# Two neighbouring rows to a partition: a matrix product with rotary embedding, rows 2p and 2p+1 of 256 in place of row 4p+r of 512

## The chip, the cores and the metric

One core of a Trainium2 chip runs the kernel. The metric is the device time of one execution in microseconds (us). Engines: PE (matmul; PEld is its loading of weights), DVE, ACT, POOL, and SP, which here only issues transfers. ACT and POOL issue transfers too; each engine works through its own instructions in order.

## The reference

x is 16 x 512 x 768 in float32, the weight 768 x 768, cos and sin 512 x 64. With 12 heads of 64 columns, the kernel computes a product and rotates it by position:

```python
y = np.matmul(x, weight)                       # (16, 512, 768)
y = y.reshape(batch, seq, n_heads, head_dim)   # head_dim 64
y1, y2 = y[..., :32], y[..., 32:]
out1 = y1 * cos1 - y2 * sin1                   # cos1, sin1: first 32 columns of cos, sin
out2 = y2 * cos2 + y1 * sin2                   # cos2, sin2: the other 32; indexed by the position in seq
out = np.concatenate([out1, out2], axis=-1).reshape(batch, seq, hidden)
```

## The kernel before

**Tiles and groups.** The 8192 rows of x are cut into 64 tiles of 128 rows, four tiles to a group, 16 groups (0 to 15, `LAST` is 15). Tile s of group g is, of batch 4*(g//4)+s, the rows 4p + g%4 for p = 0 to 127 (`where`). So all tiles of a group have the same positions and need the same row of cos and sin on each partition. A load or a store of a tile moves 128 rows of 768 floats (3 KB), each 12 KB from the next.

**From x to the product.** PE needs x transposed, in fp16. For most tiles SP loads a tile to `xs` (L210), ACT casts it to `xc` with the columns sorted into three blocks of pairs (`cast`, the copy of L190), PE transposes it through PSUM (`turn_rows`, L271; in the start-up `turn`, L256), and ACT copies the result to `xt` (L190). These are the plain tiles. In groups 5 to 13 and in group 15 the second pair of tiles of the group is a block (`BLOCKS`): four quarter loads bring 32-row pieces of it (`load_quarter`, L225) so that a transposition of 32x32 squares on DVE (`turn_pair`, L299) turns both tiles at once into `xp`. Blocks of odd groups come by SP to `xb` and are cast by ACT to `xd` (`cast_pair`); blocks of groups 6, 8, 10 and 12 come by POOL, which casts in the transfer, to `xh`, and DVE then reads them with a step of three words. PE takes the transposed tile as its weights and streams the weight matrix past it, into six PSUM banks `py` (3072 columns, one group). From tile 4 to tile 57 it works with half arrays: two streams of 64 rows each (`walk`, `one`, L362), the second 1024 columns behind the first, so that both halves of the array are busy; the start-up and the end use the whole array (L337).

**Rope.** A group's 3072 columns are cut into units: 0 to 512, 512 to 1536, 1536 to 2048, 2048 to 3072 (in the last groups into units of 512, at the very end of 256 and 128). For each unit DVE multiplies the product once with cos and once with the shifted sin (`rope`, L419; `csn` holds both, with a broadcast over the heads of a unit) and POOL adds the two halves into `ov` (L445). A finished unit frees its banks for the next group. From group 1 on POOL adds both units of a half group at once (128x1536).

**Order.** Everything is emitted in a fixed order by the loop over tiles i. At the end of step i it emits DVE's turn of a block that is due (`bturns`), PE's transposition of tile i+3 and ACT's copy of it (`turns`), ACT's cast of tile i+5 (`casts`), POOL's loads, and the stores that are due (`stores`, L477, most on ACT's queue, the last ones on SP's). `pump` emits loads on SP's queue as buffers come free: ten buffers `xs` of one tile, three of a block. Semaphores alone decide when an instruction starts; an instruction that waits holds back all behind it on its engine.

Of the kernel before, what the change touches and what calls it, by code (L numbers as in the profile page):

```python
# [10 lines left out]
FP32 = mybir.dt.float32  # L11
# [97 lines left out]
def kernel(  # L109
# [19 lines left out]
    R = 32  # L129
    NQ = P // R  # L130
    NT = H // (2 * P)
    SB = S // P
    QB = 4
    NG = B * SB // QB
# [10 lines left out]
    def sbuf(name, shape, dt):  # L145
        return nc.alloc_sbuf_tensor(name, shape, dt).ap()

    NX, NB, NBH, NC, NCP, NXT, NXP, NOV = 10, 3, 3, 5, 2, 8, 4, 4

    ident = sbuf("ident", [P, P], FP16)  # L150
    cold = sbuf("cold", [P, 512], FP16)
    sin_sb = sbuf("sin_sb", [P, SB, D], FP32)
    csn = sbuf("csn", [P, 2, SB, D], FP32)
    w_raw = sbuf("w_raw", [P, NT, 2, H], FP32)
    w_sb = sbuf("w_sb", [P, NT, 2, H], FP16)
    xs_b = [sbuf(f"xs{i}", [P, H], FP32) for i in range(NX)]
    xb_b = [sbuf(f"xb{i}", [P, 2 * H], FP32) for i in range(NB)]
    xh_b = [sbuf(f"xh{i}", [P, 2 * H], FP16) for i in range(NBH)]
    xc_b = [sbuf(f"xc{i}", [P, H], FP16) for i in range(NC)]
    xd_b = [sbuf(f"xd{i}", [P, 2 * H], FP16) for i in range(NCP)]  # L160
# [32 lines left out]
    def where(i):  # L193
        g, s = divmod(i, QB)
        return QB * (g // SB) + s, g % SB

# [7 lines left out]


    def load(i, e="sp"):
        b, r = where(i)
        k = ring("xs", NX)
        xs[i] = k
        do(e, lambda eng: eng.dma_start(  # L210
            out=xs_b[k], in_=x[b].rearrange("(p r) h -> r p h", r=SB)[r]),
            writes=[f"xs{k}"], dma=f"xs{k}")

    def load_quarter(gh, q):
        g, h = gh
        b, r = where(g * QB + 2 * h)
        e = BLOCKS[gh]
        src = x[b : b + 2].rearrange("b (j a r) (q k) -> r q a (b j) k", r=SB, a=R, q=NQ)
        if q == 0:
            xs[gh] = ring("xh", NBH) if e == "pool" else ring("xb", NB)  # L220
        k = xs[gh]
        name = f"xh{k}" if e == "pool" else f"xb{k}"
        buf = xh_b[k] if e == "pool" else xb_b[k]
        dst = buf.rearrange("p (j k) -> p j k", j=2 * NQ)
        do(e, lambda eng: eng.dma_start(out=dst[ts(q, R)], in_=src[r, q]),  # L225
           writes=[f"{name}q{q}"], dma=name)

# [13 lines left out]
    def cast(i, e):  # L241
        k = xs[i]
        c = ring("xc", NC)
        xc[i] = c
        do(e, copy(e, xc_b[c].rearrange("p (t m e) -> p t m e", t=NT, e=2),
                   xs_b[k].rearrange("p (m t e) -> p t m e", t=NT, e=2)),
           reads=[f"xs{k}"], writes=[f"xc{c}"])

    def turn(i, e):
        c = xc[i]  # L250
        k = ring("pt", 2)
        z = ring("xt", NXT)
        src = xc_b[c].rearrange("p (t m e) -> p t e m", t=NT, e=2)
        pt = pt_b[k].bitcast(FP16)[:, 0:H].rearrange("p (t e m) -> p t e m", t=NT, e=2)
        for t, h in CHUNKS:
            do("pe", lambda eng: eng.transpose(pt[:, t, h, :], src[:, t, h, :], ident),  # L256
               reads=[f"xc{c}", "ident"], writes=[f"pt{k}"], tick=(t, h) == CHUNKS[-1])
        do(e, copy(e, xt_b[z], pt), reads=[f"pt{k}"], writes=[f"xt{z}"])
        xT[i] = (lambda t, h: xt_b[z][:, t, h, :], f"xt{z}")

    def turn_rows(i, e):

        c = xc[i]
        z = ring("xt", NXT)
        src = xc_b[c].rearrange("p (t m e) -> p t e m", t=NT, e=2)
        pts = [pt_b[r].bitcast(FP16)[:, 0 : H // 2].rearrange(
            "p (t e m) -> p t e m", t=NT, e=2) for r in range(2)]
        for t, h in CHUNKS:
            for r in range(2):
                rows = ts(r, HP)  # L270
                do("pe", lambda eng: eng.transpose(  # L271
                    pts[r][:, t, h, :], src[rows, t, h, :], ident[rows, rows]),
                    reads=[f"xc{c}", "ident"], writes=[f"pt{r}"], tick=(t, h) == CHUNKS[-1])
        do(e, copy(e, xt_b[z].rearrange("p t e (r m) -> p r (t e) m", r=2),
                   pt2.bitcast(FP16)[:, :, 0 : H // 2].rearrange("p r (c m) -> p r c m", m=HP)),
           reads=["pt0", "pt1"], writes=[f"xt{z}"])
        xT[i] = (lambda t, h: xt_b[z][:, t, h, :], f"xt{z}")

    def cast_pair(gh, e="act"):
        k = xs[gh]  # L280
        c = ring("xd", NCP)
        xc[gh] = c
        do(e, copy(e, xd_b[c].rearrange("p (t j e) -> p t j e", t=NT, e=2),
                   xb_b[k].rearrange("p (j t e) -> p t j e", t=NT, e=2)),
           reads=[f"xb{k}q{q}" for q in range(NQ)], writes=[f"xd{c}"])

    def turn_pair(gh):
        g, h = gh
        z = ring("xp", NXP)
        dst = xp_b[z].bitcast(FP32)  # L290
        if BLOCKS[gh] == "pool":
            k = xs[gh]
            src = xh_b[k].bitcast(FP32).rearrange("p (j t) -> p t j", t=NT)
            rd = [f"xh{k}q{q}" for q in range(NQ)]
        else:
            c = xc[gh]
            src, rd = xd_b[c].bitcast(FP32), [f"xd{c}"]
        v = xp_b[z].rearrange("p (t m e) -> p t e m", t=NT, e=2)
        do("dve", lambda eng: eng.transpose(out=dst, in_=src), reads=rd, writes=[f"xp{z}"])  # L299
        for s in (0, 1):  # L300
            xT[g * QB + 2 * h + s] = (
                lambda t, e, s=s: v[:, t, e, ts(s, P)], f"xp{z}")

# [92 lines left out]
    def rope(g, u):  # L396
        c0, c1, ps, banks, adder = u
        w, r = c1 - c0, g % SB
        nh = w // D
        whole = 0 < g and (g, c0 // 1536) < (LAST - 4, 1)  # L400
        if adder == "dve":
# [11 lines left out]
        else:  # L413
# [4 lines left out]
            tq, keys = products(home, 512, 0, 256) if adder == "hold" else products(home, w, 0, w)  # L418
        do("dve", lambda eng: eng.tensor_tensor(  # L419
            out=tq.rearrange("p j (h d) -> p j h d", d=D),  # L420
            in0=ps.rearrange("p (h d) -> p h d", d=D)
            .unsqueeze(1).broadcast_to((P, 2, nh, D)),
            in1=csn[:, :, r, :].unsqueeze(2).broadcast_to((P, 2, nh, D)),
            op=MULT), reads=banks + ["csn"], writes=keys)
        if g not in ov_of:
# [41 lines left out]
    def store(g, c0, c1, e):  # L467

        o = ov_of[g]
        b, r = where(g * QB)  # L470
        s0, s1 = c0 // H, -(-c1 // H)
        dst = out.rearrange("b (p r) h -> r p b h", r=SB)[r, :, b + s0 : b + s1]
        src = ov_b[o].rearrange("p (b h) -> p b h", b=QB)[:, s0:s1]
        if (c1 - c0) % H:
# [3 lines left out]
           reads=[f"ov{o}c{c}" for c in range(c0, c1, 64)],  # L478
           dma=f"xs{c0 // 256 % NX}" if (c1 - c0) % H else f"ov{o}_{c0}")

# [8 lines left out]
    for k in order:  # L489
# [4 lines left out]
    do("sp", lambda eng: eng.dma_start(  # L494
        out=csn[:, 0], in_=cos.rearrange("(p r) d -> p r d", r=SB)), writes=["cos"], dma="ov3_0")
    do("sp", lambda eng: eng.dma_start(
        out=sin_sb, in_=sin.rearrange("(p r) d -> p r d", r=SB)), writes=["sin"], dma="ov3_1536")


    fetch, quarters = [], []  # L500
    soon = [p for p in sorted(BLOCKS) if BLOCKS[p] == "sp"]
    for i in range(QB, NTILE):
        if soon and i >= max(2, soon[0][0] - 1) * QB:
            quarters += [(soon[0], q) for q in (0, 2, 1, 3)]
            soon.pop(0)
        if not is_block(i):
            fetch.append(i)
            for _ in range(2 if i == QB * (LAST - 1) else 1):
                if quarters:
                    fetch.append(quarters.pop(0))  # L510
        elif quarters and quarters[0][0] == pair_of(i):
            fetch.append(quarters.pop(0))
    fetched = [0]
    xs_used, xb_used = [0], [0]
    xs_sent, xb_sent = [4], [0]

    def pump():

        while fetched[0] < len(fetch):
            j = fetch[fetched[0]]  # L520
            if isinstance(j, int):
                if xs_sent[0] - xs_used[0] >= NX:
                    return
                load(j)
                xs_sent[0] += 1
            else:
# [26 lines left out]
    def castx(i, e):  # L553
        cast(i, e)
        xs_used[0] += 1

# [21 lines left out]
    for c in CHUNKS[3:5]:  # L578
# [4 lines left out]
    do("dve", lambda eng: eng.tensor_copy(  # L583
        out=csn[:, 1, :, 0:HD], in_=sin_sb[:, :, HD:D]), reads=["sin"], writes=["csn1"])
    do("dve", lambda eng: eng.tensor_scalar_mul(
        out=csn[:, 1, :, HD:D], in0=sin_sb[:, :, 0:HD], scalar1=-1.0),
        reads=["sin", "csn1", "cos"], writes=["csn"])
    assert not quarters
    pump()
# [164 lines left out]
```

## Time and profile before

| | |
|---|---|
| three runs | 150.62, 150.62, 152.17 us; median 150.62 |
| span of the profiled execution | 148.2 us; its own time is not listed beside it, so what lies outside the span is taken from the median: 2.4 us |
| granted clock of PE | 0.998 |
| moved by the transfers | 51.67 MB in 27555 packets, 349 GB/s on the mean |
| busy share of PE, DVE, ACT, POOL | 95, 85, 53, 82% |

The span runs from the first to the last instruction. "Busy" of PE is a modelled end for each matmul, so it is not a share of its peak. In the lines of groups, the columns are: line, engine, operation, output and input with their shapes, count; then busy us in all, mean ns of one; then the idle time ahead of them and who ended it. A line number can be that of a helper: L190 is the copy for all engines. In a timeline a line has the start in us, the length in us, then what ran; neighbours on an engine overlap in the records by about 0.1 us.

Four windows, in busy us of each engine:

| window | PE | DVE | ACT | POOL | share of the DMA engines |
|---|---|---|---|---|---|
| 0 to 18 us | 14.91 | 8.18 | 9.01 | 1.99 | 0.90 |
| 18 to 52 us | 34.00 | 28.50 | 27.88 | 31.66 | 1.08 |
| 52 to 100 us | 48.00 | 45.92 | 22.63 | 45.16 | 1.12 |
| 100 to 126 us | 26.00 | 24.87 | 14.02 | 24.65 | 1.04 |
| 126 to 148.2 us | 17.89 | 18.55 | 5.51 | 18.30 | 0.81 |

Up to 18 us is the start-up, in 18 to 52 us fall groups 1 to 4, whose tiles are all plain, then come the groups with blocks; the last window is the end.

### The profile page before, as it was taken

How to read it: one execution, taken by the hardware profiler on the slowest of the kernel's cores; microseconds unless marked ns; L12 is line 12 of the kernel's file. 1: busy time of each engine (PE TensorE's matmuls, PEld its weight loads, DVE VectorE, ACT ScalarE, POOL GpSimd, SP SyncE). 2: the span in 40 equal slices, each digit the busy share in tenths (PEclk: the TensorE clock that was granted, in tenths of full speed). 3: DMA queues.
4: the chain of work that ended last, by engine and by line, in shares of the span. 5: the costliest groups of instructions: out<-in, count | busy, mean ns of one | idle time of the engine just before them, and what ended most of it. 6: DMA issues, size and time to landing. Idle time of an engine off the chain costs nothing.

```text
span 148.2 us, 4422 instructions
## 1 busy us (share of the span) xinstructions
PE 140.8 (95%) x1948; PEld 112.7 (76%) x1948; DVE 126.0 (85%) x99; ACT 79.0 (53%) x94; POOL 121.8 (82%) x73
## 2 busy tenths in 40 slices
PE   6789999999999999999999999999999999999980
PEld 2335578888888888888888888888888888765860
DVE  0335998886988899899989998999989999999991
ACT  3453898777777933557261915375263919931010
POOL 1000396999999998999999999879699999999990
PEclk9999999999999999999999999999999999999999
DMA  3999999999999999999999999999999999998675
GB/s 124 352 395 403 402 406 398 373 379 296 317 366 330 352 353 277 294 408 287 319 355 397 379 323 358 365 408 324 381 365 337 411 409 416 410 408 333 264 297 180
DMA packets 27555, 51.67 MB, mean 349 GB/s; under 512 B 6160, under 2 KB 13072, under 8 KB 27536
## 3 DMA queue, kind: packets, MB, share of 16 engines
q1 hardware_dynamic: 15824, 28.84, 57.0%
q10 hardware_dynamic: 7360, 20.97, 35.9%
q0 software_dynamic: 4352, 1.57, 8.6%
q8 instruction: 15, 0.25, 0.7%
q14 instruction: 4, 0.03, 0.1%
HBM read 27.79 MB, written 25.17 MB: 357 GB/s over the span
## 4 chain that ended last, share of the span: by engine, by line
PE 78%; DVE 12%; DMA 4%; issue 1%; SPq 1%; DVEq 0%
PE py L362 68%; DVE tq L419 8%; PE py L337 5%; PE pt L271 4%; DMA w_raw<-in_weight_dram 4%; DVE w_raw L419 2%; SPq L210 1%; PE pt L256 1%; DVE ov L445 1%; DVE xs L419 1%; SPq L232 1%; DVE w_sb L190 0%; DVEq L57 0%; SPq L749 0%; SPq L119 0%
## 5 line engine op out<-in xcount | busy, mean ns | idle before, releaser
L445 POOL TENSOR_TENSOR ov<-tq 128x512 f32<-128x512 f32 (+3 forms) x35 | 76.8, 2220 | 20.1 <-DVE tq L419 20.1
L362 PE MATMUL py<-w_sb,xt 64*128 64x256 f16 (+1 forms) x864 | 81.5, 323 | 0.0
L419 DVE TENSOR_TENSOR tq<-py,csn 128x1024 f32<-128x1024 f32 (+2 forms) x51 | 74.4, 1496 | 4.6 <-PE py L362 4.5
L362 PEld LDWEIGHTS py<-w_sb,xt 64*128 64x128 f16 x864 | 59.9, 94 | 11.1 <-DVE tq L419 0.4
L190 ACT COPY xt<-pt 128x768 f16<-128x768 f16 x42 | 33.5, 801 | 47.5 <-PE pt L271 46.3
L362 PE MATMUL py<-w_sb,xp 64*128 64x512 f16 (+1 forms) x432 | 42.7, 323 | 0.0
L190 ACT CAST xc<-xs 128x768 f16<-128x768 f32 x44 | 38.8, 911 | 6.9 <-DMA xs<-in_x_dram 6.7
L419 DVE TENSOR_TENSOR w_raw<-py,csn 128x1024 f32<-128x1024 f32 (+1 forms) x22 | 35.3, 1606 | 4.4 <-PE py L362 4.0
L445 POOL TENSOR_TENSOR ov<-w_raw 128x1536 f32<-128x1536 f32 (+2 forms) x15 | 35.4, 2374 | 1.9 <-DVE w_raw L419 1.9
L362 PEld LDWEIGHTS py<-w_sb,xp 64*128 64x128 f16 x432 | 30.7, 94 | 5.0
L337 PE MATMUL py<-w_sb,xt 128*128 128x256 f16 (+1 forms) x102 | 17.0, 317 | 1.4 <-DVE w_sb L190 1.1
L271 PEld LDWEIGHTS pt<-ident,xc 64*128 64x128 f16 x456 | 14.9, 95 | 1.3 <-issue 0.2
L337 PEld LDWEIGHTS py<-w_sb,xt 128*128 128x128 f16 x102 | 9.2, 98 | 7.4 <-DVE w_sb L190 2.7
L271 PE MATMUL pt<-ident,xc 64*128 64x64 f16 x456 | 14.7, 190 | 0.0
L190 ACT CAST xd<-xb 128x1536 f16<-128x1536 f32 x6 | 9.8, 1634 | 0.0
L225 POOL DMA_DIRECT2D xh<-in_x_dram x16 | 9.4, 591 | 0.0
L190 DVE CAST w_sb<-w_raw 128x768 f16<-128x768 f32 x6 | 3.4, 559 | 3.6 <-DMA w_raw<-in_weight_dram 3.6
L299 DVE STREAM_TRANSPOSE xp<-xd 128x768 f32<-128x768 f32 x6 | 5.8, 970 | 0.0
L190 ACT COPY ov<-py 128x256 f32<-128x256 f32 x1 | 0.4, 372 | 10.1 <-POOL ov L445 10.1
L540 PE MATMUL py<-cold 128*128 128x512 f16 x12 | 4.3, 521 | 1.4 <-DVE cold L482 1.4
L190 DVE COPY xt<-pt 128x768 f16<-128x768 f16 x2 | 1.1, 558 | 4.8 <-PE pt L256 4.8
L299 DVE STREAM_TRANSPOSE xp<-xh 128x768 f32<-128x768 f32 x4 | 4.9, 1234 | 0.0
(23 smaller groups left out, 22.6 us busy)
## 6 DMA issues: line engine op xcount, KB each, us to landing
out_dram<-ov ACTq DMA_DIRECT2D x26, 768.0 KB, 9.6
xs<-in_x_dram SPq DMA_DIRECT2D x44, 384.0 KB, 16.4
xb<-in_x_dram SPq DMA_DIRECT2D x24, 192.0 KB, 16.4
out_dram<-ov SPq DMA_DIRECT2D x4, 768.0 KB, 6.2
w_raw<-in_weight_dram SPq DMA_DIRECT2D x6, 384.0 KB, 6.9
xh<-in_x_dram POOLq DMA_DIRECT2D x16, 96.0 KB, 12.1
out_dram<-ov SPq DMA_DIRECT2D x1, 384.0 KB, 2.3
out_dram<-ov ACTq DMA_DIRECT2D x1, 384.0 KB, 2.3
```

Of the source, the lines that this page charges most:

```text
L190: eng.copy(out=o, in_=i_) if e == "act" else eng.tensor_copy(out=o, in_=i_)
L210: do(e, lambda eng: eng.dma_start(out=xs_b[k], in_=x[b].rearrange("(p r) h -> r p h", r=SB)[r]), writes=[f"xs{k}"], dma=f"xs{k}")
L225: do(e, lambda eng: eng.dma_start(out=dst[ts(q, R)], in_=src[r, q]), writes=[f"{name}q{q}"], dma=name)
L232: do(e, lambda eng: eng.dma_start(out=w_raw[:, t, h], in_=wv[t, h]), writes=[f"wr{t}{h}"], dma=f"ov{t}_0" if h else f"xb{t}")
L256: do("pe", lambda eng: eng.transpose(pt[:, t, h, :], src[:, t, h, :], ident), reads=[f"xc{c}", "ident"], writes=[f"pt{k}"], tick=(t, h) == ...
L271: do("pe", lambda eng: eng.transpose(pts[r][:, t, h, :], src[rows, t, h, :], ident[rows, rows]), reads=[f"xc{c}", "ident"], writes=[f"pt{r ...
L299: do("dve", lambda eng: eng.transpose(out=dst, in_=src), reads=rd, writes=[f"xp{z}"])
L337: do("pe", lambda eng: eng.matmul(ps, get(t, h), w_sb[:, t, h, a - s * H : z - s * H], start=start, stop=stop), reads=[key, f"w{t}{h}"], w ...
L362: do("pe", lambda eng: eng.matmul(py[:, a:z], get(t, h)[rows], w_sb[rows, t, h, a - s * H : z - s * H], start=start, stop=not opens and en ...
L419: do("dve", lambda eng: eng.tensor_tensor(out=tq.rearrange("p j (h d) -> p j h d", d=D), in0=ps.rearrange("p (h d) -> p h d", d=D) .unsque ...
L445: do(adder, lambda eng: eng.tensor_tensor(out=ov_b[o][:, ds(c0, w)].rearrange("p (h t d) -> p h t d", t=2, d=HD), in0=tq[:, 0].rearrange(" ...
L540: do("pe", lambda eng: eng.matmul(py[:, ts(b, 512)], cold[:, 0:P], cold, start=True, stop=warmed[0] < WARM - 6), reads=["cold"], writes=[f ...
```

## The change

The rows are dealt out anew. Groups 0 to 11 (`NEW` is 12) are now one batch each: tile s of group g holds the rows 256*(s//2) + 2p + s%2 of batch g. Two neighbouring tiles of a pair thus lie in memory as 128 runs of 6 KB. Groups 12 to 15 take four batches (12 to 15) and one tile of each, rows 256*u + 2p + v with u, v = divmod(g-12, 2), as groups of equal positions like before. With that come these edits:

- Pairs 6 to 23 that are no blocks (eleven pairs, tiles 12 to 45) are loaded by one transfer of 6 KB rows (`load_two`) and cast by one instruction on ACT when the second tile of the pair is due (`cast_two`). Pairs 0 to 5 and the pairs of groups 12 to 15 go tile by tile (`by_tile`), as before.
- `xs` and `xc` are buffers of a pair: six and three of them, in place of ten and five of a tile.
- The two halves of a group 0 to 11 are stored as 128 runs of 6 KB (24 stores).
- A block's quarter of groups 5 to 11 is still one transfer; of groups 12, 13 and 15 it is two. The order of rows in a block is another, and DVE's transposition writes its words with a step of 8 words (32 bytes) where it wrote them packed; PE then reads every fourth fp16 of `xp`, where it read every second.
- A unit of 1024 columns in groups 0 to 11 holds 256 columns of an even row and 768 of an odd one. `csn` gets four slots (even, odd, odd, odd) so that one instruction still does a unit; the two further slots are filled by a copy on POOL in the start-up (`csnx`).
- cos and sin are loaded as two runs of 512 B to a partition, before one of 1 KB.

The core of the diff:

```diff
-    NX, NB, NBH, NC, NCP, NXT, NXP, NOV = 10, 3, 3, 5, 2, 8, 4, 4
+    NX, NB, NBH, NC, NCP, NXT, NXP, NOV = 6, 3, 3, 3, 2, 8, 4, 4
...
-    csn = sbuf("csn", [P, 2, SB, D], FP32)
+    csn = sbuf("csn", [P, 2, 2, 4, D], FP32)
...
     def where(i):
         g, s = divmod(i, QB)
-        return QB * (g // SB) + s, g % SB
+        return (g, s) if g < NEW else (NEW + s, g - NEW)
...
+    def by_tile(pr):
+        return pr < 6 or pr >= 2 * NEW
...
+    def load_two(pr, e="sp"):
+        b, r = where(2 * pr)
+        k = xs[pr] = ring("xs", NX)
+        do(e, lambda eng: eng.dma_start(
+            out=xs_b[k], in_=x[b].rearrange("(u p v) h -> u p (v h)", p=P, v=2)[r // 2]),
+            writes=[f"xs{k}_0", f"xs{k}_1"], dma=f"xs{k}_0")
...
+    def cast_two(pr, e):
+        k = xs[pr]
+        c = xc[pr] = ring("xc", NC)
         do(e, copy(e, xc_b[c].rearrange("p (t m e) -> p t m e", t=NT, e=2),
                    xs_b[k].rearrange("p (m t e) -> p t m e", t=NT, e=2)),
-           reads=[f"xs{k}"], writes=[f"xc{c}"])
+           reads=[f"xs{k}_0", f"xs{k}_1"], writes=[f"xc{c}_0", f"xc{c}_1"])
...
     def turn_pair(gh):
...
-        dst = xp_b[z].bitcast(FP32)
+        dst = xp_b[z].bitcast(FP32).rearrange("p (t a w) -> p t w a", t=NT, a=R)
...
-        v = xp_b[z].rearrange("p (t m e) -> p t e m", t=NT, e=2)
+        v = xp_b[z].rearrange("p (t m s e) -> p t e s m", t=NT, s=2, e=2)
         do("dve", lambda eng: eng.transpose(out=dst, in_=src), reads=rd, writes=[f"xp{z}"])
         for s in (0, 1):
             xT[g * QB + 2 * h + s] = (
-                lambda t, e, s=s: v[:, t, e, ts(s, P)], f"xp{z}")
+                lambda t, e, s=s: v[:, t, e, s], f"xp{z}")
...
+        if mixed:
+            make = lambda eng: eng.tensor_tensor(
+                out=tq, in0=ps.unsqueeze(1).broadcast_to((P, 2, w)),
+                in1=csn[:, u].rearrange("p j g d -> p (j g) d")
+                .unsqueeze(2).broadcast_to((P, 8, w // 256, D)), op=MULT)
...
     def store(g, c0, c1, e):
...
+        if g < NEW:
+            dst = out[g].rearrange("(u p v) h -> u p (v h)", p=P, v=2)[c0 // (2 * H)]
+            do(e, lambda eng: eng.dma_start(out=dst, in_=ov_b[o][:, c0:c1]),
+               reads=[f"ov{o}c{c}" for c in range(c0, c1, 64)], dma=f"ov{o}_{c0}")
+            return
...
     def castx(i, e):
-        cast(i, e)
-        xs_used[0] += 1
+        if by_tile(i // 2):
+            cast(i, e)
+        elif i % 2:
+            cast_two(i // 2, e)
+        xs_used[0] += i % 2
...
+    two = csn.rearrange("p u j g d -> p (u j) g d")
+    do("pool", lambda eng: eng.tensor_copy(
+        out=two[:, :, 2:4], in_=two[:, :, 1:2].broadcast_to((P, 4, 2, D))),
+        reads=["csn"], writes=["csnx"])
```

## The prediction, on record before the changed kernel ran

> **What bounds the kernel now.** I read four views in this order: the page, the chain of waits that ended last, the groups by form, and the timelines of ACT and DVE. The page first:
>
> ```profile
> span 148.2 us, 4422 instructions
> PE 140.8 (95%) x1948; PEld 112.7 (76%) x1948; DVE 126.0 (85%) x99; ACT 79.0 (53%) x94; POOL 121.8 (82%) x73
> ...
> PE 78%; DVE 12%; DMA 4%; issue 1%; SPq 1%; DVEq 0%
> ```
>
> PE fills its line, and the chain is PE's for 78% and DVE's for 12%. The page's DMA row is full too (9 in nearly all slices), but only 4% of the chain is a transfer, and that is a load of the weights before 10 us. The chain in order of time shows where PE holds the end:
>
> ```profile
> 31.19 0.17 PE pt L271 x10
> 31.36 1.93 PE py L362 x19
> ...
> 50.49 5.86 PE py L362 x54
> ...
> 125.86 3.45 DVE tq L419 x3
> ```
>
> From 18 to 125.8 us the chain is PE without a gap: one tile of matmuls takes 1.92 to 1.96 us and a transposition 0.17 to 0.20, so a tile period is 2.13 us, or 8.15 us for a group of four of which two are transposed on PE. After 125.86 us DVE sets the end. So time is lost by anything that makes PE wait before 126 us, or DVE late after it; faster transfers gain nothing while nobody waits for them. The longest wait of ACT for x is 2.4 us, and all four such waits lie before 16 us. The rows for what the change touches:
>
> ```profile
> L190 ACT CAST xc<-xs 128x768 f16<-128x768 f32 x44 | 38.8, 911 | 6.9 <-DMA xs<-in_x_dram 6.7
> L419 DVE TENSOR_TENSOR tq<-py,csn 128x2048 f32<-128x2048 f32 x17 | 38.7, 2276 | 0.8 <-PE py L362 0.8
> ...
> L190 ACT CAST xd<-xb 128x1536 f16<-128x1536 f32 x6 | 9.8, 1634 | 0.0
> ...
> L299 DVE STREAM_TRANSPOSE xp<-xd 128x768 f32<-128x768 f32 x6 | 5.8, 970 | 0.0
> L299 DVE STREAM_TRANSPOSE xp<-xh 128x768 f32<-128x768 f32 x4 | 4.9, 1234 | 0.0
> ```
>
> **The change, part by part.** The order of PE's and of DVE's instructions stays as it was, with the same shapes apart from one; what changes is when their inputs come and how they lie.
>
> *The pair cast on ACT (cast_two).* Eleven pairs of groups 3 to 11 are cast by one instruction of 128x1536 instead of two of 128x768. The xd row has that shape and that pattern: 1634 ns against 2 x 911. ACT saves 11 x 0.19 = 2.1 us, worth nothing, since it waits 46 us for PE's transposes. But the even tile's cast moves back, to where the odd tile's stood, and so past one copy xt<-pt. The new order on ACT is: copy of tile 11, cast of 12 and 13, copy of 12, copy of 13, cast of 14 and 15, and so on. Behind the cast stands PE's next transposition, which reads its result, and behind that, in PE's order, all further matmuls. The timeline of ACT before:
>
> ```profile
> 29.32 0.80 ACT L190 COPY xt<-pt 128x768 f16<-128x768 f16 x1 [0.52 <-PE pt L271]
> 30.01 0.90 ACT L190 CAST xc<-xs 128x768 f16<-128x768 f32 x1
> 31.44 0.80 ACT L190 COPY xt<-pt 128x768 f16<-128x768 f16 x1 [0.54 <-PE pt L271]
> ```
>
> The copy of tile 11 starts at 29.32 (copies are the tiles in order, every 2.13 us). A cast starts 0.69 later, at 30.01, and with 1.63 it ends at 31.64; in the start-up PE begins 0.05 after such a cast, so at 31.69. In the timeline of PE the transposition of tile 12 begins at 31.00. PE waits 0.69 us. This happens at each pair whose first transposition follows one tile period after the last one: tiles 12, 14, 16, 18 and 20. From group 6 on the plain pair comes after two tiles that DVE turned, 5.86 us later, and the cast is hidden. 5 x 0.69 = 3.45 us, on PE's line and so on the path. The ends: 0.5 each (2.5 us) if the transposition could in truth start no earlier than 0.25 before its copy (31.19), and 0.75 each (3.75) if the weight load's head start is lost as well.
>
> *The block's transposition on DVE (turn_pair, L299 before).* The same 768 elements are written with consecutive words 32 bytes apart (t, w, a with a innermost) and not packed, ten times. No row has a hop on the written side. The nearest is xh's, which reads with a step of 12 bytes: 1234 against 970 ns, so 8 more bytes of step cost 264 ns. A gain is excluded, packed is the least. So the bounds of one instruction's extra are 0 (a written hop is free) and 264 x 28/8 = 924 ns (in proportion to the step, 28 bytes more). I take the upper, because the price rose with the distance in the only two points there are and 32 is farther out than 12: 970 + 924 = 1894 ns. For xh, which hops on the read side already, I let the longer side count: 1894 - 1234 = 660. Six and four: 6 x 0.924 + 4 x 0.660 = 8.18 us.
>
> What covers it: DVE's own idle time. A group needs two units of 2276 ns and two of half that size, 1217 ns (6.7 us by their starts) and the transposition, in 8.15 us. After each of the first eight transpositions DVE waits for PE once, for 0.54, 0.26, 0.41, 0.27, 0.54, 0.15, 0.54 and 0.28 us, 2.99 in all. After the last two there is nothing left:
>
> ```profile
> 119.17 0.97 DVE L299 STREAM_TRANSPOSE xp<-xd 128x768 f32<-128x768 f32 x1
> 120.06 1.19 DVE L419 TENSOR_TENSOR tq<-py,csn 128x1024 f32<-128x1024 f32 x1
> 121.17 3.83 DVE L419 TENSOR_TENSOR w_raw<-py,csn 128x1024 f32<-128x1024 f32 x3
> 124.95 0.98 DVE L299 STREAM_TRANSPOSE xp<-xd 128x768 f32<-128x768 f32 x1
> 125.86 6.98 DVE L419 TENSOR_TENSOR tq<-py,csn 128x1024 f32<-128x1024 f32 x6
> ```
>
> Then the units come late, PE waits for the banks that they free, and since DVE makes the end, what is not swallowed is paid in full: 8.18 - 2.99 = 5.19 us. At xh's price (0.264 each) the first eight fit and only the last two are paid, 0.5 us; at the full 0.924 for all ten it is 6.3.
>
> A page speaks against this edit. The Trainium skill, "Vector Engine (DVE) Microarchitecture Reference", section "5.2 Measured stream behaviour on trn2", has a written stream that steps 24 words each element at 2.50 ns per column against about 1.05 packed, and says that small steps cost more than large ones. By the rows the edit costs 5.19 us; by that figure an estimate is 768 x 1.45 = 1.11 us each, 8.1 us after the same idle time, and 162.5 us for the kernel. The trace agrees with its rule that a hop costs; its figure for a written one no run here shows.
>
> *Weights from xp.* PE now reads the turned block with 8 bytes between columns, 4 before. xt (packed) and xp (4 bytes) both take 94 ns in their rows, so I put 0; the other end is in the rivals.
>
> *The start.* cos and sin come in twice as many packets of half the size (512 B). DVE waited 0.2 us for sin and PE then 0.4 us for DVE, so this lies on the path. By section 3 of the page a packet cost 116 ns at a mean of 2849 B (q10: 35.9% of 16 x 148.2 us over 7360) and 85 at 1823 B (q1): 0.03 ns per byte and 31.6 ns per packet, so 256 more packets on 16 engines are 0.5 us. Bounds 0 and 0.5; I take 0.25. The wider table is filled by one POOL copy of 128x512, between 0.30 (the 128x128 cast) and 1.28 us (the 128x512 add). DVE's first unit does not read it and takes 1.2 us, and POOL has nothing else then; 0, at most 0.1 without that cover. The rope's products have the same sizes: 0.
>
> *Loads and stores.* Eleven pair loads replace 22, and 24 stores move 6 KB rows; SP has fewer issues, ACT as many. By 31.6 ns, 4480 packets less (11 x 128 and 24 x 128) free 8.9 us on each DMA engine, but nobody waits on that. On POOL's queue the block of group 12 is loaded by eight DMAs in place of four: 0 to 4 x 0.591 = 2.4 us. Behind it stand its adds, with idle gaps of 0.24, 1.51 and 1.35 us in the next 26 us; DVE waits for one only three half groups later. 0, at most 2.4.
>
> The sum: 0.25 + 3.45 + 5.19 = 8.9 us on the profiled span of 148.2, so 157.1. The execution's time outside the span is the median's 150.62 less 148.2, 2.4 us; forecast 159.5 us.
>
> **The rivals.** (a) A written hop costs what xh's read hop does, or less. For it: the nearest row, same instruction. Against: 32 bytes are not 12. 150.62 + 0.25 + 3.45 + 0.5 = 154.8 us.
>
> (b) PE's weight loads suffer from the 8-byte step. If they double to 188 ns, they are longer than the matmul of 256 columns that hides them (107 ns at the pace of 4608 columns in 1.92 us): 81 ns x 12 for each lane and block, x 10, 9.7 us. This and DVE's lateness fall in the same groups and the larger counts: 150.6 + 9.7 + 3.7 = 164.0. Against it: 94 ns at 2 and at 4 bytes alike.
>
> (c) The other side: the transfers pace the middle, and the lighter queues give it back. For it: the DMA row is full and the bytes per second dip to 277 to 330 GB/s between 30 and 60 us. Freeing 8.9 us per engine would then give 150.6 - 8.9 = 141.7 us, PE's waits for the cast vanishing in earlier loads. It decides if PE's tile period varies with the GB/s row; it is 2.13 us at 398 (22 to 26 us) and at 296 (33 to 37 us) alike.
>
> That the change does not do what it says (no fewer packets) would alter none of this, since no step rests on it.
>
> **How the numbers follow.** Forecast 0.64, with its own range 156.3 to 161.2 (extras of 0.5 each, 10 x 0.5 - 2.99 = 2.0, up to all ten at 0.924 with the dearest casts and start, 6.3 + 3.75 + 0.5); (a) 0.26; (b) 0.06; (c) 0.04. The range for 8 in 10 is 153.4 to 163: its low end is a free written hop with waits of 0.55 and a free start (150.62 + 2.75), which takes in (a); its high end goes two thirds of the way from 161.2 to (b). A change under 1% (1.5 us) can't be told from none here. Of (c), 0.03 is faster and 0.01 within 1%, where only part of it is given back; all else is slower, 0.96.
>
> **What would show it.** Right: PE's transpositions waiting for ACT xc five times near 0.7 us between 30 and 52 us; the transposition's row near 1.9 us for both sources; the units' waits for PE gone from 55 us on and PE waiting for DVE. Wrong: PE's tile period even through 30 to 52 us, or that row under 1.3 us; the weight loads' row above 100 ns would put (b) in its place.

## The result, and the profile after

The changed kernel takes 155.46 us (median of four executions, 155.27 to 156.25), the kernel before in the same comparison 150.62 (150.32 to 152.17): a ratio of 1.032, interval 1.026 to 1.039. It is slower by 4.84 us; the forecast was 159.5, so the direction held, and so did the range for 8 in 10 (153.4 to 163), but not the size. Ratios here and below leave out executions more than 1.5% above the fastest of the same kernel, so a few differ from the ratio of the medians; intervals are for 95%.

The page of the changed kernel:

```profile
span 153.5 us, 4414 instructions
PE 142.6 (93%) x1948; PEld 108.0 (70%) x1948; DVE 130.3 (85%) x99; ACT 78.3 (51%) x83; POOL 124.3 (81%) x78
...
PE 73%; DVE 9%; ACT 7%; DMA 5%; issue 2%; SPq 1%; DVEq 0%
```

The span grew by 5.3 us (from 148.2). PE's busy time grew by 1.8 and DVE's by 4.3, but what is new on the chain is ACT: it had no entry before and has 7% now. The chain in order of time shows where (start, length, what):

```profile
30.00 0.20 PE pt L305 x11
...
30.28 0.80 ACT xt L191
31.07 1.51 ACT xc L191
...
32.64 0.35 PE pt L305 x12
32.99 1.95 PE py L396 x18
...
54.69 5.85 PE py L396 x58
...
134.56 1.89 DVE tq L464 x2
```

In the kernel before this stretch was PE's alone, one transposition (pt) every 2.13 us. Here the chain leaves PE at 30.28, goes through a copy and the pair cast on ACT, and comes back at 32.64. The same loop stands in the chain four more times, with transpositions at 37.52, 42.42, 47.32 and 52.22. The long stretch of group 5 begins at 54.69, before at 50.49: 4.20 us late, of which 0.96 are a later start (PE's first half-array matmul stands at 19.01, before at 18.04) and 3.24 come from the five loops, 0.65 each. From there to 126 us PE loses no more: its groups follow each other in 8.15 us as before. The waits (who waits for whom: us in all, times, longest):

```profile
ACT xc L191 <- DMA xs<-in_x_dram: 7.7, 4, 2.7
...
PEld pt L305 <- ACT xc L191: 3.9, 6, 0.8
...
PE pt L305 <- ACT xc L191: 2.3, 5, 0.5
```

PE waits for the pair cast five times; x is waited for at the start only. The groups by form:

```profile
L396 PEld LDWEIGHTS py<-w_sb,xp 64*128 64x128 f16 x432 | 31.4, 110 | 5.2
...
L191 ACT CAST xc<-xs 128x1536 f16<-128x1536 f32 x11 | 17.9, 1628 | 0.0
...
L333 DVE STREAM_TRANSPOSE xp<-xd 128x768 f32<-128x768 f32 x6 | 9.5, 1588 | 0.0
...
L333 DVE STREAM_TRANSPOSE xp<-xh 128x768 f32<-128x768 f32 x4 | 6.4, 1600 | 0.0
```

The block's transposition takes 1588 ns from xd and 1600 from xh; it took 970 and 1234. Weight loads from xp take 110 ns, before 94. The last one on the timeline of DVE:

```profile
129.72 1.61 DVE L333 STREAM_TRANSPOSE xp<-xd 128x768 f32<-128x768 f32 x1
131.15 6.89 DVE L464 TENSOR_TENSOR tq<-py,csn 128x1024 f32<-128x1024 f32 x6
```

The unit behind it starts at 131.15, before at 125.86: 5.29 us later, 4.20 of them PE's and about 1.1 DVE's own.

### The profile page after: what moved, and what is told of

The parts are those of the page before. It is cut to its first block, busy times and chain, and to the rows that moved or that the text cites. A ratio compares the mean times of both kernels' runs of the same rounds, so it can differ in the third digit from the quotient of the medians.

```text
span 153.5 us, 4414 instructions
## 1 busy us (share of the span) xinstructions
PE 142.6 (93%) x1948; PEld 108.0 (70%) x1948; DVE 130.3 (85%) x99; ACT 78.3 (51%) x83; POOL 124.3 (81%) x78
## 2 busy tenths in 40 slices
DMA packets 23347, 51.67 MB, mean 337 GB/s; under 512 B 6176, under 2 KB 13344, under 8 KB 23328
## 4 chain that ended last, share of the span: by engine, by line
PE 73%; DVE 9%; ACT 7%; DMA 5%; issue 2%; SPq 1%; DVEq 0%
PE py L396 62%; DVE tq L464 6%; PE pt L305 5%; ACT xc L191 5%; DMA w_raw<-in_weight_dram 5%; PE py L371 4%; ACT xt L191 2%; DVE w_raw L464 2%; SPq L216 1%; PE pt L291 1%; DVE ov L490 1%; SPq L254 1%; DVE xs L464 1%; DVE w_sb L191 0%; DVEq L57 0%
## 5 line engine op out<-in xcount | busy, mean ns | idle before, releaser
L396 PEld LDWEIGHTS py<-w_sb,xt 64*128 64x128 f16 x864 | 54.8, 94 | 15.9 <-DVE tq L459 0.4
L191 ACT CAST xc<-xs 128x768 f16<-128x768 f32 (+1 forms) x33 | 37.4, 1150 | 7.8 <-DMA xs<-in_x_dram 7.7
L464 DVE TENSOR_TENSOR tq<-py,csn 128x1024 f32<-128x1024 f32 (+2 forms) x35 | 38.8, 1144 | 2.5 <-PE py L396 2.5
L459 DVE TENSOR_TENSOR tq<-py,csn 128x2048 f32<-128x2048 f32 x16 | 36.5, 2281 | 2.8 <-PE py L396 2.8
L459 DVE TENSOR_TENSOR w_raw<-py,csn 128x2048 f32<-128x2048 f32 x8 | 18.3, 2289 | 2.1 <-PE py L396 2.1
L464 DVE TENSOR_TENSOR w_raw<-py,csn 128x1024 f32<-128x1024 f32 x14 | 17.1, 1222 | 1.7 <-PE py L396 0.8
L305 PE MATMUL pt<-ident,xc 64*128 64x64 f16 x456 | 13.6, 190 | 2.3 <-ACT xc L191 2.3
L333 DVE STREAM_TRANSPOSE xp<-xd 128x768 f32<-128x768 f32 x6 | 9.5, 1588 | 0.0
L240 POOL DMA_DIRECT2D xh<-in_x_dram x12 | 7.1, 594 | 0.0
L333 DVE STREAM_TRANSPOSE xp<-xh 128x768 f32<-128x768 f32 x4 | 6.4, 1600 | 0.0
```

Of the source, the lines that this page charges most:

```text
L191: eng.copy(out=o, in_=i_) if e == "act" else eng.tensor_copy(out=o, in_=i_)
L240: do(e, lambda eng: eng.dma_start(out=buf.rearrange("p (w k) -> p w k", w=2 * NQ)[ts(q, R)], in_=src), writes=[f"{name}q{q}"], dma=name)
L305: do("pe", lambda eng: eng.transpose(pts[r][:, t, h, :], src[rows, t, h, :], ident[rows, rows]), reads=[from_, "ident"], writes=[f"pt{r}"] ...
L396: do("pe", lambda eng: eng.matmul(py[:, a:z], get(t, h)[rows], w_sb[rows, t, h, a - s * H : z - s * H], start=start, stop=not opens and en ...
L459: make = lambda eng: eng.tensor_tensor(out=tq, in0=ps.unsqueeze(1).broadcast_to((P, 2, w)), in1=csn[:, u].rearrange("p j g d -> p (j g) d" ...
L464: make = lambda eng: eng.tensor_tensor(out=tq.rearrange("p j (h d) -> p j h d", d=D), in0=ps.rearrange("p (h d) -> p h d", d=D) .unsqueeze ...
```

## The experiments

Theory: five stalls of PE behind the pair cast (3.2 us) and about 1.1 us of DVE at the end. The rival is the forecast's own sum, in which the transposition costs more than the cast. "Late x" (casts on ACT that wait for a tile of x to land) came up on the way and got a theory and rivals of its own. A packet below is one record of a DMA queue, here mostly one run of 3 or 6 KB.

### One part undone, or one alone

**Cast by tile** (e1_cast_by_tile), the changed kernel with two single casts in the old places:

```diff
-        if by_tile(i // 2):
-            cast(i, e)
-        elif i % 2:
-            cast_two(i // 2, e)
+        cast(i, e)
```

> The changed kernel, but the eleven pairs of groups 3 to 11 that one transfer loads are cast on ACT tile by tile again, each at its old place. Theory (the place and length of the pair cast make PE wait, 5 x 0.65 = 3.24 us between 30 and 53 us): 155.5 - 3.2 = 152.2 us, no wait of PE's transpositions for ACT xc above 0.2 us, tile period 2.13 us through all of 18 to 52 us. Rival (PE is held back there by the larger pair transfers or by their buffers): stays at 155.5, with the waits moved to DMA xs. If the written hop on DVE were the main cost, it would stay above 154.

Measured: median 153.28 us of seven, but from 152.07 to 157.35; ratio 1.0187 (1.0137 to 1.0236), clear of the changed kernel's. The stalls are gone: PE's tile period is 2.13 us from 24 to 51 us. The lowest execution, 152.07, is where the theory puts the time, the median is 1.1 above it. The upper end is something new. The profile is of the execution with 157.35 us, and there ACT's casts wait for x nine times; four of these waits, of 1.9 to 5.0 us, lie between 102 and 129 us, where nobody waited for x in either original.

**Packed transposition** (e2_packed), the changed kernel with the words written packed and the block's rows loaded in the order that this needs:

```diff
-        dst = buf.rearrange("p (j s k) -> p s j k", j=NQ, s=2)[ts(q, R)]
+        dst = buf.rearrange("p (s j k) -> p s j k", j=NQ, s=2)[ts(q, R)]
...
-        dst = xp_b[z].bitcast(FP32).rearrange("p (t a w) -> p t w a", t=NT, a=R)
+        dst = xp_b[z].bitcast(FP32)
```

> The changed kernel, but the rows of a block are dealt out to the partitions so that DVE's transposition writes packed words again and PE reads xp with a step of 4 bytes (the same rows come by the same number of packets). Theory (the hop costs DVE 0.62 us for xd and 0.37 for xh, which its idle time swallows up to about 124 us, and only the last two are paid): xd row 970 ns, weight loads of xp back from 110 to 94 ns, total 155.5 - 1.2 = 154.3 us. Rival (DVE's lateness is what costs most, in the whole of 55 to 126 us): 155.5 - 5.2 + 3.0 = 153.3 or less.

Measured: 154.14 us (153.50 to 154.63, five), 1.3 less than the changed kernel, or 1.0 when each is taken against the kernel before of its own call (150.28 and 150.62); the transpositions take 969 and 1236 ns again, the weight loads from xp 94. The five stalls stay.

**The written step alone** (e3_hop_only), the kernel before with one line of the change:

```diff
-        dst = xp_b[z].bitcast(FP32)
+        dst = xp_b[z].bitcast(FP32).rearrange("p (t a w) -> p t w a", t=NT, a=R)
```

> The kernel before with one edit: DVE's transposition of a block writes its words 32 bytes apart, as in the changed kernel; PE reads xp as before, so in the blocks the rows of the result are in another order. Theory: rows of 1.59 and 1.60 us, up to 124 us swallowed by DVE's idle time (10 extras are 5.2 us, 2.99 of them idle, and what is left beyond 1.2 was idle in pieces too short to be listed), so 150.6 + 1.2 = 151.8 us; by the sum of the prediction with the measured price it would be 150.6 + 2.2 = 152.8. Rival (the lateness in the changed kernel comes from its start and casts and not from the hop): 150.6.

Measured: 151.39 us against 150.28, so 1.11 (ratio 1.008, 1.0054 to 1.0107); transpositions of 1583 and 1596 ns. Ten of them cost 5.2 us more on DVE, and 1.1 arrives at the end: the price of the last two (2 x 0.61 = 1.2). With PE reading at its old 4 bytes, weight loads stay at 94 ns, so the 110 above belong to the 8-byte step and not to the transposition.

**Both undone** (e4_both), the edits of the first two runs together.

> The changed kernel with both undone: casts tile by tile, blocks packed. What is left of the change: pair loads, 6 KB stores, the wider table, the start. Theory: 150.6 plus the start, where PE began its first half-array matmul 0.96 us later: 151.0 to 151.6 us. If the start's delay was chance, 150.6. Rival (the lighter transfer queues do pace something): below 150.0.

Measured: twelve executions in two bunches, five between 150.40 and 151.93 and five between 155.03 and 156.46, with two between; ratio 1.0061 (1.0027 to 1.0095). So without the two known costs the kernel can come back to the old time, but in about half its executions it does not. What remains of the change (pair loads, 6 KB stores, halved quarters) gains nothing. The profile is of an execution with 151.05 us; two casts wait for x in it, 0.42 and 1.20 us, between 126 and 130 us, where in the kernel before none does. That late x makes the upper bunch too is likely, but no profile of it shows this.

### Is it the pair cast's place or its length?

**One tile further ahead** (e7_ahead), the changed kernel with:

```diff
-    C_AHEAD, T_AHEAD, B_AHEAD, P_AHEAD = 5, 3, 4, 20
+    C_AHEAD, T_AHEAD, B_AHEAD, P_AHEAD = 6, 3, 4, 20
```

> The changed kernel with ScalarE casting one tile further ahead of TensorE's stream, and nothing else. If the pair cast costs because the first of its two tiles is wanted earlier than the cast of both can end (its place in the order), starting each 2.1 us earlier takes away the five stalls of 0.65 us: about 152.1 us. If it costs because ScalarE spends more time in all on pairs (throughput), the stalls stay and the time with them, about 155.3 us. A third possibility is that the earlier cast then waits for its x to land, as in the cast-by-tile kernel: waits of ScalarE for xs and a time of 154 us or more.

Measured: 153.36 us (152.43 to 154.58, four), ratio 1.0172 (1.0069 to 1.0275). The stalls are gone with every pair cast still there: it is the place. The third possibility came with it, somewhat smaller than expected. Its waits and its ACT timeline:

```profile
ACT xc L191 <- DMA xs<-in_x_dram: 11.8, 6, 2.7
...
DVE xp L333 <- ACT xd L191: 1.3, 1, 1.3
```

```profile
121.52 0.92 ACT L191 CAST xc<-xs 128x768 f16<-128x768 f32 x1 [2.25 <-DMA xs<-in_x_dram]
...
125.52 0.92 ACT L191 CAST xc<-xs 128x768 f16<-128x768 f32 x1 [1.86 <-DMA xs<-in_x_dram]
...
126.33 1.59 ACT L191 CAST xd<-xb 128x1536 f16<-128x1536 f32 x1
```

Two casts wait for tiles of the last groups; the block's cast (xd) stands behind them on ACT, DVE's transposition behind that, and a copy that PE needs as well: PE stands still for 1.8 us at 127 us. In the changed kernel no cast waits for x at the end: its stalls delay PE by 3.2 us, more than the 2.3 us of the longer of these two waits, so they can have hidden this.

### Which part makes x late?

Three candidates: the pair loads (768 KB land at once, buffers come free by pairs), the block quarters in two transfers, the stores in 6 KB packets.

**Loads by tile** (f2_tile_loads), the kernel with both undone, and no pair loads either:

```diff
-            if by_tile(pr):
-                fetch.append(i)
-            elif i % 2 == 0:
-                fetch.append(("two", pr))
-                continue
+            fetch.append(i)
...
```

> The changed kernel with the cast by tile and the transposition packed (as in the kernel with both, 150.4 to 156.5 us, in two bunches), and with x of groups 3 to 11 loaded tile by tile, 3 KB packets, where the change loads two tiles at once in 6 KB packets. If the late bunch comes from the pair loads (a buffer of two tiles comes free later and 768 KB land together), all executions should lie at 150.4 to 151.5. If it comes from the quarters of the blocks that load in two transfers, or from the 6 KB stores, about half of them should still lie near 155.

Measured: 153.99 us, 152.69 to 155.34 (four). The profile is of the execution with 152.69 us:

```profile
ACT xc L191 <- DMA xs<-in_x_dram: 23.3, 14, 2.8
```

Ten of the fourteen waits come after 45 us. So x is late without any pair load.

**Halved quarters alone** (f4_halved_quarters), in the kernel before:

```diff
+        if g >= 12:
+            for s in range(2):
+                do(e, lambda eng: eng.dma_start(
+                    out=dst[ts(q, R), 4 * s : 4 * s + 4], in_=src[r, q][:, 4 * s : 4 * s + 4]),
+                   writes=[f"{name}q{q}" if s else f"{name}q{q}s"], dma=name)
+            return
...
```

> The kernel before, with the quarters of groups 12, 13 and 15 loaded in two transfers of half the size each, as the change does, and nothing else (its twelve added transfers on SP's queue and four on POOL's). If these are what makes x come late in some executions, a share of them should lie 4 to 5 us above 150.3. If the pair loads or the 6 KB stores do it, all should lie within 0.5 us of the kernel before.

Measured: 150.37 us of ten against 150.27; ratio 0.9992 (0.9944 to 1.0040), and no cast waits for x after the start. Alone they do not make x late.

**3 KB stores** (f3_small_stores), the kernel with both undone. The two rows of a store are walked in reverse on both sides, so that no packet spans both. Bytes and the order of instructions stay, but a store now takes 0.61 us or more to issue on ACT's queue, where it took 0.34 or more:

```diff
-            dst = out[g].rearrange("(u p v) h -> u p (v h)", p=P, v=2)[c0 // (2 * H)]
-            do(e, lambda eng: eng.dma_start(out=dst, in_=ov_b[o][:, c0:c1]),
+            dst = out[g].rearrange("(u p v) h -> u p v h", p=P, v=2)[c0 // (2 * H)]
+            src = ov_b[o][:, c0:c1].rearrange("p (v h) -> p v h", v=2)[:, ::-1]
+            do(e, lambda eng: eng.dma_start(out=dst[:, ::-1], in_=src),
```

> The changed kernel with the cast by tile and the transposition packed (the kernel with both), and with the stores of groups 0 to 11 in packets of 3 KB as before instead of 6 KB: the same bytes from the same instructions at the same moments. If the last x tiles come late because a store's packet of 6 KB holds a DMA engine for twice as long between two packets of x, the waits for x after 90 us go, and all executions lie at 150.4 to 151.5, as the kernel before with a start 0.7 to 0.9 us later. If the stores have no part in it, the executions spread from 150.4 to 156.5 as without this edit, and stores in q10 still land in 8.6 us from 70 us on, where those of the kernel before take 10.3.

Measured: 150.64 us, eleven executions between 150.43 and 151.48. The profile is of the one with 150.43 us:

```profile
ACT xc L191 <- DMA xs<-in_x_dram: 7.3, 5, 2.5
```

All five waits lie in the first 16 us. So with the stores in 3 KB packets the profile shows no late x, with pair loads and halved quarters still there. The upper bunch is gone as well, seven of twelve executions above 152 us against none of eleven, but these counts are from two calls on two chips, and late executions are not peculiar to 6 KB stores: in this very call five of 21 of the kernel before, whose stores move 3 KB, took 153.28 to 157.00 us. The ratios with large and small packets (1.0061 and 1.0035) have intervals that overlap. The remaining 0.3 us over the kernel before (1.0003 to 1.0066) is not traced.

### The sum closed

**The change with 3 KB stores** (g1_after_small_stores): the edit of the last run, in the changed kernel.

> The changed kernel with the stores of groups 0 to 11 in packets of 3 KB, nothing else. If the 6 KB stores cost only what x comes late, and the five stalls of the pair cast give the x loads some 3 us of slack that hides it, nothing changes: about 155.3 us. If they cost the changed kernel time of their own, it falls toward 154 us.

Measured: 155.22 us (154.98 to 155.31, four), against 150.17 before it; with 6 KB it was 155.46 against 150.62. As long as the stalls are there, the stores' packets cost nothing that shows.

**And the casts further ahead** (g2_ahead_small_stores): both edits, 3 KB stores and `C_AHEAD` 6.

> The changed kernel with the casts one tile further ahead and the stores in packets of 3 KB: pair loads, pair casts and the written step of 32 bytes are all kept. If the whole loss is the place of the pair cast, the late x behind 6 KB stores, and 1.1 us of the longer transposition at the end, the time is 150.6 (the kernel with cast by tile, packed transposition and small stores) + 1.1 = 151.7 us, without a bunch of late executions. If the pair cast has a price beside its place, it stays above 152.5.

Measured: 151.88 us (151.76 to 152.13, four), against 150.17 before it; ratio 1.0111 (1.0083 to 1.0140). Its chain is PE's again at even steps, and the waits for x are those of the start alone:

```profile
29.93 1.91 PE py L396 x17
...
32.06 1.88 PE py L396 x18
...
51.19 5.81 PE py L396 x53
```

```profile
ACT xc L191 <- DMA xs<-in_x_dram: 7.4, 4, 2.5
```

This run and the one with `C_AHEAD` 6 differ in the stores alone (their packets, the walk of their rows and the time to issue them). All four executions with 6 KB lie above all four with 3 KB, by 1.5 us at the medians, but the interval of the ratio with 6 KB is wide and takes in the other. What shows the cause is the pair of profiles: the two waits for x and PE's stop of 1.8 us stand in one and not in the other. Their DMA queues between 60 and 126 us (q1 holds SP's loads, q10 the stores; packets, MB, share of the 16 engines), first with 6 KB, then with 3 KB:

```profile
q10 hardware_dynamic: 2382, 13.06, 48.6%
q1 hardware_dynamic: 6234, 9.33, 47.2%
```

```profile
q10 hardware_dynamic: 4808, 13.92, 53.0%
q1 hardware_dynamic: 6012, 9.18, 43.2%
```

With the large store packets a packet of x takes 80.0 ns on the mean (47.2% of 16 x 66 us over 6234), with the small ones 75.9; a tile of x lands 18.5 us after its issue, against 15.6, and a store in 8.6, against 9.4. The stores go faster and x pays. The landing time alone does not make x late, though: in the same window of the kernel before a tile takes 18.1 us and no cast waits; what makes the same delay matter in one kernel and not in the other is not shown. The Trainium skill, "DMA: Bandwidth & Descriptors", section "Queues, rings and completion order", says that a DMA engine takes turns between the queues that have work for it, a whole packet at a time, and that such a packet is typically 9 to 17 descriptors. That larger store packets get a larger share would fit these rows, but no run here shows the turns, nor whether a packet of the page is a packet of the profile.

### The price of a step, and the start

**A row of steps** (e5_steps), the kernel before with another written step for each block:

```diff
-        dst = xp_b[z].bitcast(FP32)
+        st = {5: 2, 7: 4, 9: 8, 11: 12, 13: 24, 15: 3, 6: 2, 8: 4, 10: 8, 12: 24}[g]
+        dst = xp_b[z].bitcast(FP32).rearrange("p (t a w) -> p t w a", w=st, a=R)
```

> The kernel before, with each block transposition on VectorE written at another step between neighbouring words: 2, 4, 8, 12 and 24 words from the dense source xd (groups 5, 7, 9, 11, 13) and from the strided source xh (groups 6, 8, 10, 12), and 3 words for group 15; the rows of the blocks come out in another order. Measured so far: step 1 takes 0.97 us from xd and 1.23 us from xh, step 8 takes 1.59 and 1.60. If each source and each written word outside a 32-byte line costs a line, the price jumps at step 8 and stays flat after; if it grows with the step, step 24 is the slowest, 2 us or more, and step 2 near 1.1; if any step costs alike, all are near 1.6.

Measured, on DVE's timeline, from xd with steps of 2, 4, 8, 12, 24 and 3 words:

```profile
52.96 0.97 DVE L300 STREAM_TRANSPOSE xp<-xd 128x768 f32<-128x768 f32 x1
...
69.26 1.59 DVE L300 STREAM_TRANSPOSE xp<-xd 128x768 f32<-128x768 f32 x1
...
85.58 1.58 DVE L300 STREAM_TRANSPOSE xp<-xd 128x768 f32<-128x768 f32 x1
...
101.94 1.56 DVE L300 STREAM_TRANSPOSE xp<-xd 128x768 f32<-128x768 f32 x1
...
119.73 2.06 DVE L300 STREAM_TRANSPOSE xp<-xd 128x768 f32<-128x768 f32 x1
...
126.50 1.24 DVE L300 STREAM_TRANSPOSE xp<-xd 128x768 f32<-128x768 f32 x1
```

Each step is one instruction for each source. None of the three expected curves holds as a whole; of the second its far end does (24 words, over 2 us). Two words are free, three cost 0.27 us, four to twelve all 0.6, twenty-four 1.1. From xh, which is read at three words, steps of 2, 4, 8 and 24 take 1.23, 1.59, 1.60 and 2.08: the dearer side counts, and the other adds nothing.

**The rows read at the start** (s1_start), the kernel before with the changed kernel's rows in its first twelve loads:

```diff
-            out=xs_b[k], in_=x[b].rearrange("(p r) h -> r p h", r=SB)[r]),
+            out=xs_b[k], in_=x[b].rearrange("(p r) h -> r p h", r=SB)[r] if i >= 12 else
+            x[i // 4].rearrange("(u p v) h -> u v p h", p=P, v=2)[i % 4 // 2, i % 2]),
```

> The kernel before, with its first twelve tile loads reading the rows that the changed kernel reads there (groups 0 to 2 from one batch each, at 6 KB steps, where the kernel before reads four batches at 12 KB steps); the rows of these groups come out in other places. TensorE's first half-array matmul began at 18.04, 18.14, 18.14 and 18.88 us in the four profiles that read the old rows, and at 18.67 to 19.46 us in six that read the new ones. If the rows read make the late start, it begins at about 19.0 us here and the time is 151.1 us; if it is chance or another part of the change (the table's transfers, the buffers), it begins at about 18.1 and the time is 150.3 us.

Measured: the profile began late, at 18.80, but the median of eleven is 150.41 against 150.33 (ratio 1.0016, 0.9986 to 1.0046). A late start can come without these rows too: the kernel before with the written step alone began at 18.88. On its chain the load of weights that PE first waits for took 7.21 us, in the changed kernel 7.17, in the kernel before 6.35, which is 0.8 of the 0.96 us. So the difference at the start can't be charged to these rows. The nine profiles with the changed kernel's start began at 18.52 to 19.46, the four with the old start at 18.04 to 18.88; later on the whole, for a cause that stays open.

## Why the prediction was right in direction and wrong in size

| step | predicted, us | measured, us | from |
|---|---|---|---|
| pair cast, PE's five waits | 3.45 | 3.34 | 155.22 less 151.88: the cast one tile ahead, with 3 KB stores in both |
| transposition at 32 bytes | 5.19 | 1.0 to 1.4 | 1.11 alone; 0.98 by undoing it in the changed kernel; 1.40 between the last run (1.71 over the kernel before) and the one with both undone and 3 KB stores (0.31), which also differ in the casts |
| start | 0.25 | 0.3 | what is left with all else undone; not traced |
| sum | 8.9 | 4.84 | the two medians |

**The pair cast: right, in place and price.** The step said that the transposition of tile 12 would begin at 31.69 instead of 31.00; in the changed kernel it begins at 32.64, which less the later start of 0.96 is 31.68. Five stalls, at the tiles named.

**The transposition: the mechanism was right, two terms were mis-sized.** First the price. Of the bounds 0 and 0.924 the step took the upper, by a straight line through the steps of 1 and 3 words. Measured are 0.62 from xd and 0.37 from xh, because the price does not rise in proportion: it is flat from 4 to 12 words. The ten cost 6 x 0.62 + 4 x 0.37 = 5.2 us in all, not 8.18. Second the cover. With these prices and the listed idle time of 2.99 us the step's own formula would still give 2.2. The measured 1.1 is just the last two, so the first eight were swallowed whole. The timelines account for it. The step counted the units by their starts but the transposition by its length, and behind the longer one the next unit starts with more overlap. From start to start it takes 1.43 us from xd (129.72 to 131.15), before 0.91 (124.95 to 125.86), and 1.43 from xh (65.19 to 66.62), before 1.15 (60.99 to 62.14). That is 0.52 to 0.54 and 0.28 us more: 3.2 for the first eight, 1.05 for the last two. And an instruction that need not wait starts about 0.1 us before the recorded end of the one ahead, so a wait that goes frees 0.1 more than it lists, 0.8 for eight; 2.99 + 0.8 = 3.8 us cover 3.2. This is worked out, not tried. It also means that DVE's groups just about fill PE's 8.15 us now; the timeline lists no wait of DVE for PE in them any more, as forecast, but PE never waited for DVE either, where the prediction expected it to.

From the figure of the Trainium skill ("Vector Engine (DVE) Microarchitecture Reference", "5.2 Measured stream behaviour on trn2") an estimate of 1.11 us for each had been worked out. At the 24 words that the page speaks of, the row of steps shows 1.09; at this kernel's 8 words it is 0.62. The figure agrees here at 24 words. The page also says that small steps cost more than large ones, and its large ones are of 4 KiB, which no run here has; from 2 to 24 words the price only rises.

**Outside the span.** The forecast added 2.4 us, the median less the span. In every execution whose own time is listed beside its span, 1.73 to 1.85 us lay outside. So the profiled execution of the kernel before took about 150.0 us, 0.6 less than the median. The forecast is no worse for it, since it comes to the median plus 8.9 all the same; but the profiles compare a short execution before with an ordinary one after, which accounts for most of the gap between the 5.3 us of the profiles and the 4.84 of the medians.

**Weights from xp: costed at nothing, and hidden, though they did get slower.** The row went from 94 to 110 ns, over the 100 at which the prediction wanted rival (b) in its place. It does not: PE's period for a group stayed 8.15 us, and the run with 151.88 us has these loads too. 110 ns is about the 107 at which the matmul of 256 columns was put, so they are at the edge of what hides them; that is read from the two numbers and was not tried. The sign was set too low: it should have been PE's period.

**Loads and stores: costed at nothing, and nothing it was in the changed kernel** (155.46 and 155.22 with large and small store packets), but only under the cover of the stalls. With those away the 6 KB stores make x late: 153.36 us against 151.88, with casts waiting up to 2.3 us in the profile. The prediction named no such cost; it took larger packets for a saving that nobody needed.

**The rivals.** (a), 154.8 us, comes nearer than the forecast: it had the price too low (0.264) and what is paid right in kind, the last two alone. The result lies below the forecast's own range (156.3 to 161.2). (c) is refuted: with both costs undone and the packets as few as in the changed kernel, the lowest of twelve executions is 150.40 us, where the kernel before has 149.81 in the same call.

## What to carry to other kernels

Two casts made one are cheaper on the engine and can still cost time: ask when the first half of the result is wanted, and start the large instruction one step earlier. Larger packets on a queue that is not waited for can take time from the queue that is (here 75.9 ns became 80.0 for a packet of x), so look at the loads when stores grow. And when a stall is taken away, look for what it had been hiding.

## What the runs showed of the hardware that was not expected

- DVE's transposition of 128x768 words has steps in its price, not a slope: 0.97 us at 1 and 2 words, 1.24 at 3, 1.56 to 1.60 at 4, 8 and 12, 2.06 at 24. A step of 3 words costs the same on the side that reads (1.23) as on the side that writes (1.24), and of two sides the dearer one counts.
- A weight load of 64x128 fp16 takes 94 ns with columns 2 or 4 bytes apart and 110 with 8.
- Fewer packets freed nothing. The prediction put 31.6 ns on each packet; with 27555 packets q1 and q10 took 92.9% of 148.2 us, 137.7 us on each DMA engine, and with 23347 they took 90.4% of 153.5, 138.8.
